# A two-layer transformer trunk: layer 1's projections in products of 256 columns, and an earlier wide product in layer 0

## The chip, the cores and the metric

The kernel runs on one core of a Trainium2 chip. TensorE (PE) does the matrix products, VectorE (DVE) and ScalarE (ACT) prepare their operands and finish their results, GpSimd (POOL) does small powers and sums, and SyncE (SP) issues the loads. The metric is the device time of one execution in microseconds (us); three runs of the kernel before gave a median of 558.01 us (557.69 to 558.17).

## The reference

Two layers over 256 tokens of width 1024, in float32. Layer 0 is a latent attention with a rotary key, layer 1 a block attention with a relative bias; each is followed by a squared-ReLU MLP:

```python
for i in range(DEPTH):                     # DEPTH = 2
    h = rms_norm(x, attn_norm[i])
    x = x + (mla_mixer(h, ...) if i % 2 == 0 else moba_mixer(h, w_qkv, ...))
    h = rms_norm(x, mlp_norm[i])
    x = x + sq_relu_mlp(h, w_in[i], w_out[i])     # relu(h @ w_in)**2 @ w_out

# moba_mixer, layer 1: all 256 tokens are one block, so it is causal attention with a bias
qkv = (h @ w_qkv).reshape(B, S, 3, 8, 128)
q, k = rms_norm(qkv[:, :, 0], q_norm), rms_norm(qkv[:, :, 1], k_norm)
out = attention(q, k, qkv[:, :, 2], rel_bias) @ w_o
```

## The kernel before

**Three products for one.** Every float32 operand is split into a rounded high part and a low remainder, and `mm3` multiplies high by high, low by high and high by low into the same PSUM bank. For weights the split is the work of two engines: `hi` makes the high part `wh` with a copy on ACT (line 169), `lo` subtracts it from the loaded weights on DVE and gives `wl` (line 178). `hTh` and `hTl` are the two parts of a layer's input h, transposed; `aT` those of the attention's output.

**Units and the ring.** The weights come as 185 units of up to 128x1024 in one fixed order. A unit is loaded by SP into one of 4 raw buffers, then split; `wh` and `wl` have 7 buffers each. `done(i)` says that unit i has been read for the last time, and `hi` goes no further than unit `used + 7`: where the ring is full, `hi` does nothing, and the `lo` that would follow has nothing to do either. `fill(n)` is `lo(n)` and then `hi(n)`. `unit(i)` splits on demand what is not split yet. Since a program's order on an engine is the order in which the code is written, where a `fill` stands decides what is queued behind the split on DVE and ACT.

**Layer 1's projections.** q, k and v are made in two halves of four heads each, so there are six groups, k0, q0, v0, k1, v1 and q1, of four units each, and each group has two rows, one for 128 tokens. A row is 24 products of 128x512 into one bank: eight k of the contraction by the three terms, with a part of h as the stationary operand and a part of the unit as the moving one. The two rows of k0 run side by side over k, with a `fill` at each second k and a `done` behind it. q0's first row follows directly, then `tok_sums` (four products of 2 columns, the tokens' sums of squares), q0's second row, transposes of k0, and so on: from there on, transposes or attention products stand between most rows. After `tok_sums` DVE and POOL make the tokens' scale, the roots of each head's sum of squares (POOL, line 270) and the normalised rows (DVE, line 352).

**Wide products.** `wider` makes the first product of some groups 258 columns wide instead of 256, the two more going into unused columns of the bank. A group gets one where TensorE has done another type of product before it (in the MLP), and output column block 5 of each attention (`(d, h) == (5, 0)`, line 646). The attention's output projection goes by column blocks d: blocks 0 to 3 are accumulated head by head (`o`), block 4 in pieces between them, blocks 5 to 7 at the end (`col`). Its last part is written as

```python
        o(6)
        fill()
        col(4, [4, 5, 6])
        o(7)
        col(4, [7])
        for d in range(5, KD):
            col(d, range(H))
```

Of the kernel before, what the change touches and what calls it, by code (L numbers as in the profile page):

```python
# [18 lines left out]
P = 128  # L19
# [4 lines left out]
S = 256  # L24
NT = S // P
KD = D // P
H = 8
# [33 lines left out]
def trunk(ctx: ExitStack, tc: tile.TileContext, A, out):  # L61
# [9 lines left out]
    def ps():  # L71
        return psum.tile([P, 512], F32, name="ps", tag="ps")
# [11 lines left out]
    def mm(o, a, b, start, stop):  # L84
        nc.tensor.matmul(o, a, b, start=start, stop=stop)  # L85

    def mm3(o, a, b, start, stop, wide=None, between=None):

        for i, (w, t) in enumerate(((0, 0), (1, 0), (0, 1))):
            if wide and i == 0:  # L90
                mm(wide[0], a[w], wide[1], start, False)
            else:
                mm(o, a[w], b[t], start and i == 0, stop and i == 2)
            if between and between[0] == i:
                between[1]()
# [7 lines left out]
    def wider(bank, b):  # L103
        moved[0] = True
        return bank[:, :S + 2], flat(b[:, :2])[:, :S + 2]
# [8 lines left out]
    def flat(ap):  # L114
        return ap.rearrange("p a b -> p (a b)")
# [20 lines left out]
    Q0 = len(units)  # L136
# [24 lines left out]
    def hi(n=1, eng=nc.scalar):  # L161

        for _ in range(n):
            i = len(his)
            if i < min(used[0] + RING, len(units)):
                load_raw()
                w = units[i][1]
                his.append(wsp.tile([P, 1024], F32R, name="wh", tag="wh"))
                (eng.copy if eng is nc.scalar else eng.tensor_copy)(his[i][:, :w], raws[i][:, :w])  # L169

    def lo(n=1, eng=nc.vector):

        for _ in range(n):
            i = len(los)
            if i < len(his):
                w = units[i][1]
                los.append(wsp.tile([P, 1024], F32R, name="wl", tag="wl"))
                eng.tensor_sub(los[i][:, :w], raws[i][:, :w], f32(his[i][:, :w]))  # L178
                load_raw()

    def fill(n=1):
        lo(n)
        hi(n)
# [7 lines left out]
    def unit(i):  # L191
        while len(his) <= i:
            hi()
        while len(los) <= i:
            lo()
        return his[i], los[i]

    def done(i):

        used[0] = max(used[0], i + 1)  # L200

    def part(u, sl):
        return u[0][:, sl], u[1][:, sl]
# [6 lines left out]
    x = const.tile([P, KD, S], F32)  # L210
# [72 lines left out]
    def hT(k, sl=slice(None)):  # L283
        return hTh[:, k, sl], hTl[:, k, sl]

    class SumSquares:


        def __init__(self):
            self.tot = work.tile([P, 2, S], F32, name="ssum", tag="ssum", bufs=1)  # L290
            self.prev = None
# [38 lines left out]
    class Norm:  # L330
# [19 lines left out]
        def rows(self, tok):  # L350
            self.y = t2(self.nh, self.width)
            nc.vector.scalar_tensor_tensor(self.y, self.p.rearrange("p (a b) -> p a b", b=self.width), tok,
                                           self.rs[:, :, None].to_broadcast([P, self.nh, self.width]),
                                           op0=OP.mult, op1=OP.mult)
# [201 lines left out]
    class Head:  # L556


        def __init__(self, hd, aT, h, bias, extra=None):
            self.aT = (aT[0][:, h], aT[1][:, h])  # L560
            self.two = aT[0][:, :2]
            self.i = h % HG
            self.hd = hd[h // HG]
            self.h, self.bias, self.extra = h, bias, extra
# [28 lines left out]
        def turn(self):  # L593
            pt = ps()
            for i in range(3):
                nc.tensor.transpose(pt[:, i * P:(i + 1) * P], self.p[:, i * P:(i + 1) * P], ident)  # L596
            self.pT = work.tile([P, 3 * P], F32, name="pT", tag="pT", bufs=3)
            nc.scalar.copy(self.pT, pt[:, :3 * P])
# [15 lines left out]
    def out_residual(a, d, gname):  # L614
        nc.vector.tensor_add(x[:, d], a, x[:, d])
        make_h_filled(d, gname)

    def run_heads(hs, proj, post, rows, turn, mid, base, gname, n1):

        A_ = [h.logits for h in hs]  # L620
        W_ = [h.weights for h in hs]
        B_ = [h.turn for h in hs]
        C_ = [h.values for h in hs]
        accs = []

        def o(h, ds=range(4)):
            u = unit(base + h // 2)
            for d in ds:
                if h == 0:
                    accs.append(ps()[:, :S])  # L630
                c = (h % 2) * 512 + d * P
                mm3(accs[d], part(u, slice(c, c + P)), hs[h].aT, h == 0, h == H - 1)
                if h == H - 1:
                    out_residual(accs[d], d, gname)
            if h % 2:
                done(base + h // 2)

        late = {}

        def col(d, hh):  # L640
            if d not in late:
                late[d] = ps()
            u = unit(base + d)
            for h in hh:
                mm3(late[d][:, :S], part(u, slice(h * P, (h + 1) * P)), hs[h].aT, h == 0, h == H - 1,
                    wider(late[d], hs[h].two) if (d, h) == (5, 0) else None)
            if hh[-1] == H - 1:
                done(base + d)
                out_residual(late[d][:, :S], d, gname)

        if mid is not None:
            proj("k1", 0)
            fill(n1)
            post("k1", 0)
            mid()
            proj("k1", 1)
            lo(n1)
            rows("k1", 0)
            hi(n1)
            post("k1", 1)  # L660
        A_[0]()
        proj("v1", 0)
        if mid is not None:
            lo(n1)
            rows("k1", 1)
        W_[0]()
        hi(n1)
        post("v1", 0)
        turn("k1", 0)
        A_[1]()  # L670
        if mid is None:
            rows("k1", 1)
        B_[0]()
        proj("v1", 1)
        lo(n1 + (mid is None))
        W_[1]()
        hi(n1)
        post("v1", 1)
        turn("k1", 1)
        C_[0]()  # L680
        A_[2]()
        B_[1]()
        proj("q1", 0)
        lo(n1)
        W_[2]()
        hi(n1)
        post("q1", 0)
        C_[1]()
        A_[3]()
        B_[2]()  # L690
        proj("q1", 1)
        lo(n1)
        W_[3]()
        rows("q1", 0)
        hi(n1)
        post("q1", 1)
        C_[2]()
        B_[3]()
        o(0)
        fill()  # L700
        turn("q1", 0)
        rows("q1", 1)
        C_[3]()
        o(1)
        fill()
        turn("q1", 1)
        o(2, range(2))
        A_[4]()
        o(2, range(2, 4))
        W_[4]()  # L710
        A_[5]()
        lo()
        o(3)
        B_[4]()
        hi()
        W_[5]()
        A_[6]()
        col(4, [0, 1])
        C_[4]()
        B_[5]()  # L720
        W_[6]()
        A_[7]()
        lo()
        col(4, [2, 3])
        C_[5]()
        B_[6]()
        hi()
        W_[7]()
        o(4)
        fill()  # L730
        C_[6]()
        B_[7]()
        o(5)
        fill()
        C_[7]()
# [7 lines that stand above are left out]
# [9 lines left out]
    open_p = {}  # L752
# [81 lines left out]
    heads_ctx, hd, aT = head_tiles(0)  # L834
# [16 lines left out]
    for o, a, b in rope_halves(m[:, :, 0], m[:, :, 1]):  # L851
        a, b = (i[:, :, None, :].to_broadcast([P, NT, 2, HALF]) for i in (a, b))
# [221 lines left out]
    for i, bs in enumerate(pairs):  # L1074
        at = 5 * i + 9
# [13 lines left out]
    order1 = {"k0": 0, "q0": 1, "v0": 2, "k1": 3, "v1": 4, "q1": 5}  # L1089
# [18 lines left out]
        tk = slice(t * P, (t + 1) * P)  # L1108
        to_T(norms[name, t].y, hd1[int(name[1])][name[0]][:, :, tk], gqk[:, 1:2] if name[0] == "q" else None)

    def proj1_k(name, t, p, k):
        b = Q0 + 4 * order1[name]
        tk = slice(t * P, (t + 1) * P)
        mm3(p, hT(k, tk), part(unit(b + k // 2), slice((k % 2) * 512, (k % 2 + 1) * 512)), k == 0, k == KD - 1)

    def proj1(name, t):
        p = ps()
        for k in range(KD):
            proj1_k(name, t, p, k)
        if t == NT - 1:  # L1120
            done(Q0 + 4 * order1[name] + 3)
        open_p[name, t] = p

    for t in range(NT):
        open_p["k0", t] = ps()
    for k in range(KD):
        for t in range(NT):
            proj1_k("k0", t, open_p["k0", t], k)
        if k % 2:
            fill()  # L1130
            done(Q0 + k // 2)
    total = sums1[0].total()
    for t in range(NT):
        post1("k0", t, False)
    proj1("q0", 0)
    ss3 = small.tile([P, 1, NT], F32, name="ss3", bufs=1)
    tok_sums(ss3, [total], ps())
    r3[0] = row_scale("3", ss3[:, 0])
# [99 lines left out]
```

## Time and profile before

| what | value |
|---|---|
| median of three runs | 558.01 us |
| profiled execution, its own time | 558.17 us |
| its span, first to last instruction | 556.4 us |
| granted TensorE clock, mean over the span | 1.000 |
| TensorE busy | 551.4 us (99%) |
| DVE, ACT, POOL busy | 394.2, 303.3, 93.9 us |

The span is what the trace covers; the execution's own time is 1.8 us more. Matmuls overlap in the pipeline, so the time from one start to the next tells their pace, not the duration that stands in a row.

### The profile page before, as it was taken

What the parts mean: (1) busy time and instruction counts of PE and PEld (TensorE: products, weight loads), DVE (VectorE), ACT (ScalarE), POOL (GpSimd) and SP (SyncE); (2) the same over time, 40 slices, a digit from 0 to 9 for tenths busy, and PEclk for the clock granted to TensorE, in tenths of its full rate; (3) what the DMA queues carried; (4) which work ended last, traced back from release to release, by engine and by line L of the source; (5) the groups of instructions that cost most, each with busy time, mean ns of one, the idle gap of its engine ahead of it and who ended that gap; (6) DMA issues with size and microseconds to landing.
All of it is one profiled execution on the core that took longest, in us unless ns stands there. A gap on an engine that the chain in (4) does not pass through costs nothing.

```text
span 556.4 us, 10756 instructions
## 1 busy us (share of the span) xinstructions
PE 551.4 (99%) x4324; PEld 524.8 (94%) x4324; DVE 394.2 (71%) x654; ACT 303.3 (55%) x495; POOL 93.9 (17%) x108
## 2 busy tenths in 40 slices
PE   9999999999999999999999999999999999999997
PEld 6878999999999999999988888999999999999997
DVE  5998777688997689866668356777867653977630
ACT  5899675674533365435365465746856442655420
POOL 3892100032132000012133100000130311000100
PEclk9999999999999999999999999999999999999999
DMA  8833534686567376645455544344865764565800
GB/s 298 299 126 117 152 119 157 193 274 196 180 201 214 120 219 195 198 149 182 155 186 186 185 160 149 118 152 121 266 219 183 235 193 148 188 201 181 285 29 29
DMA packets 29186, 99.57 MB, mean 179 GB/s; under 512 B 3824, under 2 KB 4720, under 8 KB 29136
## 3 DMA queue, kind: packets, MB, share of 16 engines
q1 hardware_dynamic: 28656, 97.94, 54.5%
q0 software_dynamic: 336, 0.92, 0.4%
q8 instruction: 34, 0.56, 0.4%
q14 instruction: 16, 0.13, 0.1%
q10 hardware_dynamic: 144, 0.02, 0.0%
HBM read 97.82 MB, written 1.05 MB: 178 GB/s over the span
## 4 chain that ended last, share of the span: by engine, by line
PE 96%; DVE 1%; DMA 1%; SPq 1%; ACT 0%; issue 0%; DVEq 0%
PE ps L85 93%; PE ps L372 2%; DMA x<-in_xT 1%; PE ps L596 1%; DVE wl L178 1%; SPq L158 0%; SPq L230 0%; PE ps L512 0%; DVE hTl L280 0%; ACT hTh L279 0%; ACT wh L169 0%; SPq L234 0%; DVE t L1064 0%; DVE rr L408 0%; DVE rr L416 0%
## 5 line engine op out<-in xcount | busy, mean ns | idle before, releaser
L178 DVE TENSOR_TENSOR wl<-raw,wh 128x1024 fp32r<-128x1024 f32 x177 | 218.0, 1248 | 34.5 <-ACT wh L169 34.1
L169 ACT CAST wh<-raw 128x1024 fp32r<-128x1024 f32 x177 | 182.6, 1046 | 72.4 <-PE ps L85 55.4
L85 PE MATMUL ps<-a,wh 128*128 128x256 f32 x1024 | 175.0, 276 | 0.0
L85 PEld LDWEIGHTS ps<-a,wh 128*128 128x128 f32 x1024 | 154.5, 188 | 0.0
L85 PE MATMUL ps<-hTl,wh 128*128 128x256 f32 x512 | 141.7, 277 | 0.0
L85 PE MATMUL ps<-a,wl 128*128 128x256 f32 x512 | 141.7, 277 | 0.0
L85 PE MATMUL ps<-hTh,wl 128*128 128x256 f32 x512 | 141.4, 276 | 0.0
L85 PE MATMUL ps<-hTh,wh 128*128 128x256 f32 x512 | 141.3, 276 | 0.0
L85 PEld LDWEIGHTS ps<-hTl,wh 128*128 128x128 f32 x512 | 96.1, 188 | 0.1
L85 PEld LDWEIGHTS ps<-hTh,wh 128*128 128x128 f32 x512 | 96.1, 188 | 0.1
L85 PEld LDWEIGHTS ps<-a,wl 128*128 128x128 f32 x512 | 96.1, 188 | 0.0
L85 PEld LDWEIGHTS ps<-hTh,wl 128*128 128x128 f32 x512 | 96.1, 188 | 0.0
L931 ACT ACTIVATE t<-ps 128x512 f32<-128x512 f32 (+1 forms) x34 | 19.5, 572 | 63.5 <-PE ps L85 63.5
L85 PE MATMUL ps<-aT,wh 128*128 128x256 f32 (+1 forms) x256 | 50.4, 288 | 0.0
L933 DVE SCALAR_TENSOR_TENSOR t<-ps,t 128x512 f32<-128x512 f32 (+1 forms) x34 | 22.4, 659 | 36.5 <-ACT t L931 36.3
L85 PE MATMUL ps<-wh,hTh 128*128 128x512 f32 (+2 forms) x128 | 46.0, 386 | 0.2 <-ACT wh L169 0.2
L85 PE MATMUL ps<-wl,hTh 128*128 128x512 f32 (+2 forms) x128 | 45.2, 378 | 0.4 <-DVE wl L178 0.4
L85 PE MATMUL ps<-wh,hTl 128*128 128x512 f32 (+2 forms) x128 | 45.0, 377 | 0.0
L85 PEld LDWEIGHTS ps<-aT,wh 128*128 128x128 f32 x256 | 40.4, 188 | 0.2
L85 PE MATMUL ps<-aT,wl 128*128 128x256 f32 x128 | 35.6, 278 | 0.0
L609 ACT ACTIVATE hTh<-x,gains 128x256 fp32r<-128x256 f32 x24 | 12.2, 510 | 42.3 <-POOL x L1055 25.8
L270 POOL TENSOR_TENSOR hrs<-hss,mhalf 128x4 f32<-128x4 f32 (+1 forms) x18 | 23.2, 1297 | 65.4 <-DVE hss L347 48.8
(167 smaller groups left out, 624.2 us busy)
## 6 DMA issues: line engine op xcount, KB each, us to landing
raw<-in_w_in_mlp SPq DMA_DIRECT2D x64, 512.0 KB, 4.4
raw<-in_w_out_mlp SPq DMA_DIRECT2D x64, 512.0 KB, 4.3
raw<-in_w_qkv SPq DMA_DIRECT2D x24, 512.0 KB, 3.8
raw<-in_w_u SPq DMA_DIRECT2D x8, 512.0 KB, 6.1
win<-in_w_in SPq DMA_DIRECT2D x8, 352.0 KB, 5.5
raw<-in_w_o0a SPq DMA_DIRECT2D x4, 512.0 KB, 3.9
raw<-in_w_o0b SPq DMA_DIRECT2D x4, 512.0 KB, 3.5
raw<-in_w_o1a SPq DMA_DIRECT2D x4, 512.0 KB, 4.0
```

The lines of the kernel that those rows point to most:

```text
L85: nc.tensor.matmul(o, a, b, start=start, stop=stop)
L169: (eng.copy if eng is nc.scalar else eng.tensor_copy)(his[i][:, :w], raws[i][:, :w])
L178: eng.tensor_sub(los[i][:, :w], raws[i][:, :w], f32(his[i][:, :w]))
L270: nc.gpsimd.tensor_tensor(dst, t, mhalf[:, :n].rearrange("p (a b) -> p a b", b=t.shape[-1]) if len(t.shape) == 3 else mhalf[:, :n], op=OP.pow)
L372: nc.tensor.transpose(pt[:, i * P:(i + 1) * P], yf[:, i * P:(i + 1) * P], ident)
L596: nc.tensor.transpose(pt[:, i * P:(i + 1) * P], self.p[:, i * P:(i + 1) * P], ident)
L609: nc.scalar.activation(hTh[:, k], x[:, k], AF.Copy, scale=gain(gname, k))
L931: nc.scalar.activation(rl, src, AF.Relu)
L933: nc.vector.scalar_tensor_tensor(sq, src, 0.0, rl, op0=OP.max, op1=OP.mult)
```

## The change

Each product of 512 columns in layer 1's projections becomes two of 256, with the same stationary part and the two halves of the same bank. In the first rows, k0's pair and q0's first, one product (of k = 3, with the low part of h) is taken out of its place: its first half is done in seventh place and is 258 columns wide, its second half has the other 254 and comes last. Since that last one still reads k0's second unit, `done` for k0's second and third unit moves to the end of the k0 rows. In layer 0 alone, the wide product of column block 5 is gone; block 4 has two, for head 0 (the first of the block) and for head 5 (the fourth product of its piece for heads 4, 5 and 6). Layer 1's attention keeps the wide product of block 5.

```diff
-            self.two = aT[0][:, :2]
+            self.two = aT[0][:, h:h + 2] if h < H - 1 else None
...
+                wide = d == 4 and h in (0, 5) if mid is None else (d, h) == (5, 0)
                 mm3(late[d][:, :S], part(u, slice(h * P, (h + 1) * P)), hs[h].aT, h == 0, h == H - 1,
-                    wider(late[d], hs[h].two) if (d, h) == (5, 0) else None)
+                    wider(late[d], hs[h].two) if wide else None)
...
-        mm3(p, hT(k, tk), part(unit(b + k // 2), slice((k % 2) * 512, (k % 2 + 1) * 512)), k == 0, k == KD - 1)
...
+    def proj1_row(todo, wide=False):
+        kick, rest = (todo[0][:2] + (3, 1, half) if wide else None for half in range(2))
+        if wide:
+            todo = [x for x in todo if x not in (kick, rest)]
+            todo = todo[:6] + [kick] + todo[6:] + [rest]
+        last = {x[:2]: x for x in todo}
+        for x in todo:
+            name, t, k, i, half = x
+            c0, c1 = (0, S + 2) if x == kick else (S + 2, 2 * S) if x == rest else (half * S, (half + 1) * S)
+            w = unit(Q0 + 4 * order1[name] + k // 2)[i // 2][:, (k % 2) * 512 + c0:(k % 2) * 512 + c1]
+            mm(open_p[name, t][:, c0:c1], hT(k, slice(t * P, (t + 1) * P))[i % 2], w, (k, i, half) == (0, 0, 0),
+               x == last[name, t])
+            yield
...
-    for k in range(KD):
-        for t in range(NT):
-            proj1_k("k0", t, open_p["k0", t], k)
-        if k % 2:
+    row = [("k0", t, k, i, half) for k in range(KD) for t in range(NT) for i in range(3) for half in range(2)]
+    for at, _ in enumerate(proj1_row(row, True), 1):
+        if at % 24 == 0:
             fill()
-            done(Q0 + k // 2)
+            if at in (24, 96):
+                done(Q0 + at // 24 - 1)
...
-    proj1("q0", 0)
+    proj1("q0", 0, True)
```

On TensorE, at the start of the k0 rows, before (`ps_3610` is the last bank of layer 0's MLP, `ps_3692` and `ps_3693` are the banks of k0's two rows, `wh_3484` is k0's first unit):

```order
L85 MATMUL ps_3610<-a1_1324,wh_3448 128x256
L85 MATMUL ps_3692<-wh_3484,hTh_156 128x512
L85 MATMUL ps_3692<-wh_3484,hTl_157 128x512
L85 MATMUL ps_3692<-wl_3486,hTh_156 128x512
L85 MATMUL ps_3693<-wh_3484,hTh_156 128x512
```

and of the change (`wh_3524` is k0's second unit):

```order
L85 MATMUL ps_3610<-a1_1324,wh_3448 128x256
L85 MATMUL ps_3692<-wh_3484,hTh_156 128x256 x2
L85 MATMUL ps_3692<-wh_3484,hTl_157 128x256 x2
L85 MATMUL ps_3692<-wl_3486,hTh_156 128x256 x2
L85 MATMUL ps_3692<-wh_3524,hTl_157 128x258
L85 MATMUL ps_3693<-wh_3484,hTh_156 128x256 x2
```

Each product has become two, and the wide one stands seventh. There are 288 products of 512 columns before and 576 of half the width in the change.

On DVE, from the sums of the tokens on (`ss3`), before; `wl_3813` is the second unit of v0, `wl_3857` and `wl_3903` are its third and fourth, and its first stands in the k0 rows already; the three L352 are the normalised rows of k0, k0 and q0, and the second L343 belongs to q0's second row:

```order
L316 COPY ss3_3796<-ps_3797 128x2
L347 TENSOR_SCALAR hss_3768<-hss_3768,sq3_3805 128x4
L178 TENSOR_TENSOR wl_3813<-raw_3669,wh_3760 128x1024
L343 TENSOR_REDUCE hss_3820<-t2_3819 128x4
L347 TENSOR_SCALAR hss_3820<-hss_3820,sq3_3805 128x4
L352 SCALAR_TENSOR_TENSOR t2_3851<-ps_3692,rs_3_3803,hrs_3807 128x512
L352 SCALAR_TENSOR_TENSOR t2_3853<-ps_3693,rs_3_3803,hrs_3810 128x512
L352 SCALAR_TENSOR_TENSOR t2_3855<-ps_3771,rs_3_3803,hrs_3823 128x512
L178 TENSOR_TENSOR wl_3857<-raw_3722,wh_3817 128x1024
L343 TENSOR_REDUCE hss_3866<-t2_3865 128x4
L347 TENSOR_SCALAR hss_3866<-hss_3866,sq3_3805 128x4
L178 TENSOR_TENSOR wl_3903<-raw_3740,wh_3861 128x1024
```

and of the change, where `wl_3943`, `wl_3947`, `wl_3999` and `wl_4015` are v0's four units:

```order
L316 COPY ss3_3860<-ps_3861 128x2
L347 TENSOR_SCALAR hss_3808<-hss_3808,sq3_3869 128x4
L343 TENSOR_REDUCE hss_3882<-t2_3881 128x4
L347 TENSOR_SCALAR hss_3882<-hss_3882,sq3_3869 128x4
L352 SCALAR_TENSOR_TENSOR t2_3937<-ps_3692,rs_3_3867,hrs_3871 128x512
L352 SCALAR_TENSOR_TENSOR t2_3939<-ps_3693,rs_3_3867,hrs_3874 128x512
L352 SCALAR_TENSOR_TENSOR t2_3941<-ps_3811,rs_3_3867,hrs_3885 128x512
L178 TENSOR_TENSOR wl_3943<-raw_3639,wh_3877 128x1024
L178 TENSOR_TENSOR wl_3947<-raw_3669,wh_3879 128x1024
L343 TENSOR_REDUCE hss_3956<-t2_3955 128x4
L347 TENSOR_SCALAR hss_3956<-hss_3956,sq3_3869 128x4
L178 TENSOR_TENSOR wl_3999<-raw_3746,wh_3951 128x1024
```

Two `fill`s of the k0 rows find the ring full, so v0's first two subtractions stand behind the three normalised rows instead of in the k0 rows and in front of the reduction, and all of the units after them come up to two places later in DVE's order.

On TensorE in layer 0's output projection, of the change (`ps_1032` is block 4, `ps_892` the first of the next four):

```order
L85 MATMUL ps_904<-aT1_478,wh_912 128x256
L85 MATMUL ps_1032<-aT0_477,wh_943 128x256
L85 MATMUL ps_1032<-aT0_477,wl_992 128x256
L85 MATMUL ps_1032<-aT1_478,wh_943 128x256
L85 MATMUL ps_1032<-aT0_477,wh_943 128x258
L85 MATMUL ps_1032<-aT0_477,wl_992 128x256
```

Before, all of these are 128x256, and the first of 258 comes 21 products further on, as the first into block 5's bank.

## Rows read from the trace of the kernel before

**Rows 1.** The page: busy time, granted clock in 40 slices, the chain by engine.

```profile
PE 551.4 (99%) x4324; PEld 524.8 (94%) x4324; DVE 394.2 (71%) x654; ACT 303.3 (55%) x495; POOL 93.9 (17%) x108
...
PEclk9999999999999999999999999999999999999999
...
PE 96%; DVE 1%; DMA 1%; SPq 1%; ACT 0%; issue 0%; DVEq 0%
```

**Rows 2.** TensorE in order of time, layer 0's last output blocks: start, duration, what.

```profile
81.20 0.28 PE L85 MATMUL ps<-aT,wl 128*128 128x256 f32 x1
...
85.09 0.28 PE L85 MATMUL ps<-aT,wl 128*128 128x256 f32 x1
...
85.79 0.28 PE L85 MATMUL ps<-aT,wl 128*128 128x256 f32 x1
...
93.27 0.28 PE L85 MATMUL ps<-aT,wl 128*128 128x256 f32 x1
```

**Rows 3.** Groups of instructions: TensorE's products of 258 columns, with their counts.

```profile
L85 PE MATMUL ps<-a,wh 128*128 128x258 f32 x4 | 1.1, 280 | 0.0
...
L85 PE MATMUL ps<-hTh,wh 128*128 128x258 f32 x3 | 0.8, 280 | 0.0
...
L85 PE MATMUL ps<-aT,wh 128*128 128x258 f32 x2 | 0.6, 280 | 0.0
```

**Rows 4.** TensorE in order of time: first of k0's rows, tok_sums, q0's second row.

```profile
271.70 0.39 PE L85 MATMUL ps<-wh,hTh 128*128 128x512 f32 x1
...
288.49 0.50 PE L85 MATMUL ps<-ones,ssum 128*128 128x2 f32 x4
288.85 0.48 PE L85 MATMUL ps<-wh,hTh 128*128 128x512 f32 x1
```

**Rows 5.** TensorE in order of time: the transposes of k0, v0's first row.

```profile
294.53 1.03 PE L372 MATMUL ps<-ident,t 128*128 128x128 f32 x8
295.32 0.48 PE L85 MATMUL ps<-wh,hTh 128*128 128x512 f32 x1
```

**Rows 6.** TensorE in order of time: two stretches of 256 columns after other products.

```profile
75.08 0.28 PE L85 MATMUL ps<-aT,wl 128*128 128x256 f32 x1
...
75.42 0.28 PE L85 MATMUL ps<-aT,wl 128*128 128x256 f32 x1
...
76.54 0.36 PE L85 MATMUL ps<-aT,wh 128*128 128x256 f32 x1
...
78.04 0.81 PE L85 MATMUL ps<-pT,v 128*128 128x256 f32 x4
```

**Rows 7.** DVE in order of time, from the k0 rows to v0's first row.

```profile
280.83 4.39 DVE L178 TENSOR_TENSOR wl<-raw,wh 128x1024 fp32r<-128x1024 f32 x3 [0.97 <-ACT wh L169]
...
290.67 1.21 DVE L178 TENSOR_TENSOR wl<-raw,wh 128x1024 fp32r<-128x1024 f32 x1
...
292.82 0.75 DVE L352 SCALAR_TENSOR_TENSOR t<-ps,rs,hrs 128x512 f32<-128x512 f32 x1
...
294.74 0.75 DVE L352 SCALAR_TENSOR_TENSOR t<-ps,rs,hrs 128x512 f32<-128x512 f32 x1 [0.23 <-POOL hrs L270]
295.41 1.22 DVE L178 TENSOR_TENSOR wl<-raw,wh 128x1024 fp32r<-128x1024 f32 x1
296.54 0.68 DVE L343 TENSOR_REDUCE hss<-t 128x4 f32<-128x512 f32 x1
...
297.39 1.22 DVE L178 TENSOR_TENSOR wl<-raw,wh 128x1024 fp32r<-128x1024 f32 x1
```

**Rows 8.** POOL in order of time: the first root, then the other two.

```profile
290.71 2.08 POOL L270 TENSOR_TENSOR hrs<-hss,mhalf 128x4 f32<-128x4 f32 x1 [0.54 <-DVE hss L347]
...
292.73 1.98 POOL L270 TENSOR_TENSOR hrs<-hss,mhalf 128x4 f32<-128x4 f32 x2
```

**Rows 9.** DVE and TensorE in order of time, block 4 of layer 1's output projection.

```profile
356.45 1.22 DVE L178 TENSOR_TENSOR wl<-raw,wh 128x1024 fp32r<-128x1024 f32 x1
...
357.56 0.28 PE L85 MATMUL ps<-aT,wl 128*128 128x256 f32 x1
```

More of the change, by code (lines that the diff above doesn't have):

```diff
@@ L1109, in turn1, with proj1 @@
         to_T(norms[name, t].y, hd1[int(name[1])][name[0]][:, :, tk], gqk[:, 1:2] if name[0] == "q" else None)
-    def proj1_k(name, t, p, k):
-        b = Q0 + 4 * order1[name]
-        tk = slice(t * P, (t + 1) * P)
-        mm3(p, hT(k, tk), part(unit(b + k // 2), slice((k % 2) * 512, (k % 2 + 1) * 512)), k == 0, k == KD - 1)
-    def proj1(name, t):
-        p = ps()
-        for k in range(KD):
-            proj1_k(name, t, p, k)
+    def proj1_row(todo, wide=False):
[11 more added lines that the diff above has]
+            yield
+    def proj1(name, t, wide=False):
+        open_p[name, t] = ps()
+        for _ in proj1_row([(name, t, k, i, half) for k in range(KD) for i in range(3) for half in range(2)], wide):
+            pass
         if t == NT - 1:
             done(Q0 + 4 * order1[name] + 3)
-        open_p[name, t] = p
     for t in range(NT):
         open_p["k0", t] = ps()
-    for k in range(KD):
-        for t in range(NT):
-            proj1_k("k0", t, open_p["k0", t], k)
-        if k % 2:
+    row = [("k0", t, k, i, half) for k in range(KD) for t in range(NT) for i in range(3) for half in range(2)]
+    for at, _ in enumerate(proj1_row(row, True), 1):
+        if at % 24 == 0:
             fill()
-            done(Q0 + k // 2)
+            if at in (24, 96):
+                done(Q0 + at // 24 - 1)
     total = sums1[0].total()
```

## The prediction

> **What bounds the kernel now.** I read the page first: TensorE works 99% of the span at a granted clock of 1.0 in all 40 slices, and 96% of the chain that ended last is TensorE's [rows 1]. So the change is worth what it does to the spacing of TensorE's products, and every wait that it puts into their stream counts in full; time saved on another engine counts nothing. Next I took TensorE in order of time and looked at starts only, since durations overlap. Products of 256 columns have two paces. In layer 0's last output blocks, the 33 products from 81.20 to 85.09 take 3.89 us, 117.9 ns each; the 66 from 85.79 to 93.27 take 7.48, 113.3 ns each [rows 2]. Between the two stands a product of 258 columns. The trace has nine of them (4 + 3 + 2) [rows 3], and I looked at each: from the second product behind it on the pace is 113.3 every time, and it stays through changes of bank, operand and part of the MLP until another type of product comes. Behind one the pace is 117.9: 12 products from 76.54 to 78.04 take 1.50 us, a first gap of 0.20 and eleven of 0.118. One short stretch, from 75.08 to 75.42, has three in 0.34 without any wide product in front [rows 6]; of some 25 stretches it is the only one. Products of 512 have one pace: 72 of them, from 271.70 to 288.49, take 16.79 us, 233.2 ns each [rows 4]. So two of 256 save 6.5 ns against one of 512 at the quick pace and lose 2.6 at the slow one. Last I read DVE and POOL around layer 1's first rows, because the weights' subtractions move there.
>
> **The change part by part.** The sum is made on the profiled execution, 558.17 us, of which 556.4 are the span; it lies 0.16 above the median, 558.01.
>
> *Layer 0's wide product.* It stands in 16th place behind the last other product instead of 37th, in a stream that was slow and that the nine cases say will turn quick. 21 products x 4.6 ns = 0.10 us less. The other new one, first in block 4, has five products behind it before another type comes: 0.02 at most, taken as nothing. Both read two columns of the next head's output, which the same products' neighbours read already, so they wait for nothing new.
>
> *k0's rows and q0's first row.* 72 products of 512 become 144. The stream before k0 is the MLP's, quick since its last wide product, and k0's first product waits for nothing there. 144 x 113.3 ns = 16.32, and some 0.03 for two wide products and their rests of 254: 16.35 against 16.79, 0.44 less. What a wide product does in a stream that is quick already, no row shows: all nine came in slow ones. Bounds: nothing, or the pace is lost for the rest of k0 (89 x 4.6 ns = 0.41 more), until q0's own, then in a slow stream, brings it back. I take nothing, since nothing but another type of product ever ended the quick pace. k0's wide product needs the second unit a few us early; it was split before the row begins.
>
> *The other nine rows.* q0's second, v0, k1, v1 and q1 with two each. One row takes 5.68 us now, from 288.85 to 294.53 [rows 4, 5]. As 48 products behind other work, with a first gap of 0.20 and 47 x 117.9 ns, it takes 5.74: 0.06 more, nine times 0.56. The other bound is the quick pace, 0.20 + 47 x 113.3 = 5.53, 0.15 less per row. These rows have activations as the stationary part and use each twice running, which no 256-column row of the trace does; I take the slow end, which all but one of the stretches show.
>
> *The subtractions.* Before, v0's first unit is subtracted in the k0 rows, the third of a run of three [rows 7], and its second between the roots. In the change both stand behind the three normalised rows, so I count from tok_sums, T (288.49 before). There the first root on POOL begins at T + 2.22 and takes 2.08, the other two 1.98 together, 1.0 each [rows 8]. Beside the long one runs the subtraction of v0's second unit, 290.67 to 291.88 [rows 7]; 1.0 us after its end the root is done. I read it as a root held up by DVE, so that without this subtraction it takes 1.0 too. The Trainium skill says so as well: a DVE instruction with two SBUF inputs contends with a GpSimd instruction that reads SBUF, and the second to start blocks ("SBUF — State Buffer", Who interferes with whom); the trace's 2.08 against 1.0 agrees.
>
> Then the roots end at T + 5.14, the third normalised row starts 0.03 later, and the first subtraction 0.67 behind it (294.74 to 295.41 [rows 7]), at T + 5.84. It takes 1.22, two in a row start 1.14 apart: ready at 7.06 and 8.20. TensorE reaches v0 at T + 0.36 + 5.74 + 0.79 (eight transposes [rows 5]) = 6.89, and its fifth product, the first that reads a remainder, at 7.45: 0.4 of slack. The third unit comes behind the reduction of q0's second row, 0.85 from its start to the subtraction's (296.54 to 297.39 [rows 7]): started at 8.11 + 0.85 = 8.96, ready at 10.18, wanted 24 products after the first, at 10.28. The fourth is ready at 11.31, wanted at 11.69. So nothing to 0.3 us of waiting; I take 0.05. Queued behind these on DVE are q0's second row, wanted only after k1's first, and the remainders of k1, ready some 5 us early by the same count. SP's loads for k1 go out behind the subtractions that free the raw buffers, and k1 is some 19 us behind T: no cost. On ACT two splits move behind the squares of k0, which therefore run earlier; nobody waits for either.
>
> *One more place.* The units stay a place behind until the MLP. In layer 1's output projection the subtraction from 356.45 on is then that of block 4, whose second product starts at 357.56 [rows 9]: ready at 357.67, with a start behind it 0.15 late.
>
> Sum: -0.10 - 0.44 + 0.56 + 0.05 + 0.15 = +0.22, so 558.39 on the profiled execution and 558.23 on the median. I forecast 558.3 us.
>
> **The rivals.** *The products don't turn quick* (the change doesn't do what it says): k0 and q0 run at 117.9, 144 x 117.9 = 16.98 in place of 16.35, or k0 alone loses the pace. The total is 558.7 to 558.9. For it: the operands' new roles, a wide product in a quick stream; against: nine of nine.
> The Trainium skill's spacing of N/2.4 + 2.5 ns ("TensorE: Matmul & The Clock Gate", Back-to-back issue gap) speaks for it: every halved product would cost 2.5 ns more, 288 x 2.5 = 0.72 us, estimated from that page. The rows have 20 ns over 512 columns' own 213.3 and not 2.5, so it doesn't hold here.
>
> *All nine other rows run quick.* Then they save 9 x 0.15 = 1.35 in place of losing 0.56; TensorE comes to v0's third unit at T + 9.95, 0.25 before it is ready, so the wait is 0.29. 558.01 - 0.10 - 0.44 - 1.35 + 0.29 + 0.15 = 556.6. For it: one stretch that turned quick by itself, and stationary parts used twice; against: all the others.
>
> *v0 waits for its remainders* (slower). If the first root takes 2.08 whatever runs beside it, the three subtractions come 1.08 later: the first is ready at T + 8.14, 0.7 after TensorE wants it, and the third another 0.3 later than wanted, 1.0 in all. The total is 559.2 to 559.3. It decides once the first subtraction ends later than T + 7.45. For it: the order has put them there, and 0.4 us is a small margin; against: the other two roots took 1.0.
>
> **How the numbers follow.** About 0.2% (1.1 us) is what a measurement of this kernel can tell from no change. The forecast has 0.50, the slow products 0.21, quick rows 0.14, the wait at v0 0.15. The first two lie within 0.2%; the third is faster by 0.25%; the fourth is slower by 0.22%, near the line, and may stay inside. So faster 0.14, same 0.73, slower 0.13. The forecast's own range is 557.8 to 558.7; the range reaches to the quick rows at 556.6 and to v0's wait at 559.3.
>
> **What would show it.** In the changed profile: products from k0's first to tok_sums at 113.3 ns, 16.35 us in all; rows of 5.74 us behind transposes; the pace in layer 0 turning behind block 4's wide product; a first root of 1.0 us; TensorE without a gap in v0's first row; a gap of 0.15 at block 4 of layer 1. I am wrong if a row behind transposes takes 5.53, if the wide product ends the quick pace, or if DVE shows in TensorE's waits in v0.

## The result and the profile after

The changed kernel takes 564.48 us (564.11 to 564.61, four runs); the kernel before, beside it, 557.85 (557.57 to 558.17). The ratio is 1.0117 [1.0102, 1.0131]: 6.6 us slower, where 0.3 slower was forecast and the range ended at 559.3. The profiled execution of the change took 564.11 us, its span 562.3.

The page of the changed kernel answers to [rows 1]: busy time, granted clock in 40 slices, the chain by engine.

```profile
PE 557.0 (99%) x4612; PEld 543.8 (97%) x4612; DVE 394.7 (70%) x654; ACT 302.4 (54%) x495; POOL 90.5 (16%) x108
...
PEclk9999999999999999999999999999999999999999
...
PE 96%; DVE 1%; DMA 1%; SPq 1%; issue 0%; ACT 0%; DVEq 0%
```

No share here shows the 6 us: no lower clock, no new wait in the chain, TensorE at 99% as before. So the time is in the pace of the products again, and that is read from starts.

TensorE of the change in order of time, layer 0's last output blocks (start, duration, what), answers to [rows 2]:

```profile
80.94 0.28 PE L85 MATMUL ps<-aT,wl 128*128 128x256 f32 x1
...
82.35 0.28 PE L85 MATMUL ps<-aT,wl 128*128 128x256 f32 x1
...
82.70 0.28 PE L85 MATMUL ps<-aT,wl 128*128 128x256 f32 x1
...
92.91 0.28 PE L85 MATMUL ps<-aT,wl 128*128 128x256 f32 x1
```

12 products take 1.41 us ahead of the wide one (between the second row and the third), 117.5 ns each; 90 take 10.21 behind it, 113.4. It turns the stream in its new place, as forecast.

The same view of layer 1's first rows and of block 4 of its output projection, for [rows 4, 5, 9]:

```profile
271.33 0.40 PE L85 MATMUL ps<-wh,hTh 128*128 128x256 f32 x2
...
272.04 0.28 PE L85 MATMUL ps<-wh,hTl 128*128 128x258 f32 x1
...
282.15 0.28 PE L85 MATMUL ps<-wh,hTl 128*128 128x254 f32 x1
...
282.97 0.28 PE L85 MATMUL ps<-wh,hTl 128*128 128x258 f32 x1
...
287.75 0.50 PE L85 MATMUL ps<-ones,ssum 128*128 128x2 f32 x4
288.11 0.49 PE L85 MATMUL ps<-wh,hTh 128*128 128x256 f32 x2
...
293.67 1.04 PE L372 MATMUL ps<-ident,t 128*128 128x128 f32 x8
294.46 0.48 PE L85 MATMUL ps<-wh,hTh 128*128 128x256 f32 x2
...
297.61 0.40 PE L85 MATMUL ps<-wh,hTl 128*128 128x256 f32 x2
298.03 0.51 PE L85 MATMUL ps<-wl,hTh 128*128 128x256 f32 x2
298.38 0.40 PE L85 MATMUL ps<-wh,hTh 128*128 128x256 f32 x2
...
355.92 0.47 PE L85 MATMUL ps<-aT,wh 128*128 128x256 f32 x1
356.39 0.39 PE L85 MATMUL ps<-aT,wl 128*128 128x256 f32 x1
356.61 0.40 PE L85 MATMUL ps<-aT,wh 128*128 128x256 f32 x2
...
364.78 0.36 PE L85 MATMUL ps<-aT,wh 128*128 128x256 f32 x1
```

and of the kernel before, around the second product of block 4 in [rows 9]:

```profile
357.25 0.47 PE L85 MATMUL ps<-aT,wh 128*128 128x256 f32 x1
...
357.68 0.40 PE L85 MATMUL ps<-aT,wh 128*128 128x256 f32 x2
...
365.93 0.36 PE L85 MATMUL ps<-aT,wh 128*128 128x256 f32 x1
```

k0's rows and q0's first take 16.42 us (271.33 to 287.75) in place of 16.79. q0's second row, behind `tok_sums`, takes 5.56 (288.11 to 293.67) in place of 5.68. In v0's first row two pairs of products start 0.42 apart, where the others stand 0.24 apart: a wait of 0.18 at the first use of the third unit's remainder, 298.03. The next pair follows after 0.35, 0.11 more, so the wait costs 0.29. At block 4 the first and second product stand 0.47 apart, before 0.31, and the second and third 0.22, before 0.12: a wait that costs 0.27. By the start of the last long stretch the change is ahead: its first product stands at 364.78, before at 365.93. Of these 1.15 us, 0.29 are there already at the first edited product (71.48, before 71.77); that much differs between profiled executions of the same products too, so the edits have gained 0.86.

Then it loses everything. The table by stretches (us, TensorE's busy time and number of products, and so on to the granted clock, DMA share and GB/s), first of the kernel before:

```profile
380.00:415.00 35.00, 35.00 (x311) 35.00 (x310) 25.46 (x32) 23.26 (x34) 6.65 (x4) 1.00 0.67 217
420.00:550.00 130.00, 130.00 (x1149) 130.00 (x1148) 78.57 (x88) 54.19 (x62) 11.81 (x15) 1.00 0.54 174
```

and of the change:

```profile
380.00:415.00 35.00, 35.00 (x299) 35.00 (x299) 24.33 (x29) 23.00 (x33) 6.56 (x4) 1.00 0.64 211
420.00:550.00 130.00, 130.00 (x1106) 130.00 (x1106) 79.09 (x88) 54.73 (x62) 10.31 (x14) 1.00 0.56 173
```

The same stretch of time, the same work, a granted clock of 1.00 in both, and 43 products fewer in 130 us. With two products taken off that already run at the start of a stretch, the pace is 113.3 ns before and 117.8 in the change. The wide products of layer 1's block 5 (at 369.11) and of its MLP (at 417.60) are both there, and neither turns the stream. I call these two the late wide products from here on, and say that one works where it turns the stream. 403 + 1198 products x 4.45 ns = 7.1 us lost, 1.15 gained up to there: 6.0 net, where the two profiled executions differ by 5.94.

### The profile page after: what moved, and what is told of

It reads as the page before. It is cut to its first block, busy times and chain, and to the rows that moved or that the text cites. A ratio compares the mean times of both kernels' runs of the same rounds, so it can differ in the third digit from the quotient of the medians.

```text
span 562.3 us, 11331 instructions
## 1 busy us (share of the span) xinstructions
PE 557.0 (99%) x4612; PEld 543.8 (97%) x4612; DVE 394.7 (70%) x654; ACT 302.4 (54%) x495; POOL 90.5 (16%) x108
## 4 chain that ended last, share of the span: by engine, by line
PE 96%; DVE 1%; DMA 1%; SPq 1%; issue 0%; ACT 0%; DVEq 0%
PE ps L85 93%; PE ps L372 1%; DMA x<-in_xT 1%; PE ps L596 1%; DVE wl L178 1%; SPq L158 0%; SPq L230 0%; PE ps L512 0%; DVE hTl L280 0%; ACT wh L169 0%; ACT hTh L279 0%; SPq L234 0%; DVE t L1066 0%; DVE rr L408 0%; PE ps L882 0%
## 5 line engine op out<-in xcount | busy, mean ns | idle before, releaser
L85 PE MATMUL ps<-a,wh 128*128 128x256 f32 x1024 | 178.5, 278 | 0.0
L85 PE MATMUL ps<-aT,wh 128*128 128x256 f32 x256 | 50.7, 289 | 0.0
L85 PE MATMUL ps<-wh,hTh 128*128 128x256 f32 (+2 forms) x224 | 45.7, 289 | 0.5 <-DVE wh L446 0.5
L85 PE MATMUL ps<-wl,hTh 128*128 128x256 f32 (+2 forms) x224 | 45.0, 285 | 0.4 <-DVE wl L178 0.4
L85 PE MATMUL ps<-wh,hTl 128*128 128x256 f32 (+2 forms) x224 | 45.0, 285 | 0.0
L85 PEld LDWEIGHTS ps<-wh,hTh 128*128 128x128 f32 x224 | 34.4, 188 | 1.1 <-ACT hTh L279 1.0
L85 PEld LDWEIGHTS ps<-wl,hTh 128*128 128x128 f32 x224 | 34.5, 188 | 1.0 <-DVE wl L178 0.9
```

## The experiments

Three theories at first. *Place in the program*: a wide product works or not by where its instruction stands, and 288 more products moved it. *Late units*: the ring, one unit behind since k0's rows, makes the weights late. *Phase*: a slow stream has an inner rhythm, and a wide product turns it only where it hits it rightly.

**Layer 0's edit alone.** The kernel before, with

```diff
-            self.two = aT[0][:, :2]
+            self.two = aT[0][:, h:h + 2] if h < H - 1 else None
...
+                wide = d == 4 and h in (0, 5) if mid is None else (d, h) == (5, 0)
...
-                    wider(late[d], hs[h].two) if (d, h) == (5, 0) else None)
+                    wider(late[d], hs[h].two) if wide else None)
```

> The kernel before with only layer 0's two new wide products. Theories of the 6.1 us that the changed kernel lost (its two wide products in layer 1's block 5 and in layer 1's MLP left the stream at 118 ns, where before they turned it to 113.3). Phase: a wide product turns the slow stream only if the stream meets it in a certain phase, set by what TensorE did since it last stood still; this edit moves what comes behind by 0.1 us, and the later wide products may work or not, each on its own: 557.8 if all work, about 560 if layer 1's block 5 alone fails (409 products x 4.6 ns = 1.9), about 563 if the MLP's alone fails (1198 x 4.6 ns = 5.5). Place in the program: no instruction more than before, so all work: 557.8 us. Late units: the ring is as before, all work: 557.8 us. So 557.8 says nothing against any, and takes layer 0's edit out of the causes.

558.14 us against 558.17, ratio 0.9999 [0.9989, 1.0008]. Both late wide products work. Layer 0's edit is not the cause.

**Layer 1's rows alone.** The change, with

```diff
-                wide = d == 4 and h in (0, 5) if mid is None else (d, h) == (5, 0)
+                wide = (d, h) == (5, 0)
```

> The changed kernel with layer 0's wide product put back into block 5. Phase: layer 0's edit comes 290 us ahead of the failing place, and layer 1's rows lie between; the two late wide products fail as in the change, 564.5 us, or one of them works again (562.6 with block 5 turned, 559.0 with the MLP turned), or both (about 557). Place in the program: the same 578 more instructions as in the change, both fail: 564.5 us. Late units: the ring lags as in the change, both fail: 564.5 us. If both work, the cause is something that layer 0's edit carries along.

564.34 us, ratio 1.0109 [1.0093, 1.0126]: the whole loss comes with the rows.

**The rows without their wide products.** The change, with

```diff
-    for at, _ in enumerate(proj1_row(row, True), 1):
+    for at, _ in enumerate(proj1_row(row), 1):
...
-            if at in (24, 96):
-                done(Q0 + at // 24 - 1)
+            done(Q0 + at // 24 - 1)
...
-    proj1("q0", 0, True)
+    proj1("q0", 0)
```

> The changed kernel without the wide products of k0's and q0's rows, with each unit given free where it was before, so that the ring does not fall behind. Late units: the two late wide products work again, about 557 us (or 557.5 if k0's rows stay at 118 ns). Place in the program: still 576 more instructions than before, both fail: 564.5 to 565 us. Phase: the start of the late stretch moves by some tenths of a us, so either may turn: 557, 559, 562.6 or 564.5 us. k0's rows tell as well whether they turn quick by themselves: 16.3 us from k0's first product to the tokens' sums if so, 17.0 if not.

557.51 us, ratio 0.9987 [0.9977, 0.9996]. Both late wide products work, with as many products in front of them as in the change: place in the program, as a count of products, falls. Late units and phase stand. k0's rows and q0's first take 16.97 us here, so without a wide product they stay slow.

**More wide products.** The change, with

```diff
-                wide = d == 4 and h in (0, 5) if mid is None else (d, h) == (5, 0)
+                wide = d == 4 and h in (0, 5) if mid is None else d > 4 and h == 0
...
-                    if k == f == 0 and not moved[0]:
+                    if k == f == 0 and (not moved[0] or (l, r) == (1, 0) and j < 4):
```

> The changed kernel with more wide products in layer 1: the first product of blocks 6 and 7 besides block 5, and the first product of the first four groups of the MLP's second part. Phase: each further one meets the stream in another phase, and one of them will turn it: about 557.2 us or below, and the stream stays quick from there on even where another wide product follows. Place in the program: they stand at other places, and some may work too, so 557 to 564. Late units: the weights are on time by blocks 6 and 7, and these work: about 557.2. If all fail, 564.5 us, and it is not the phase of single wide products.

564.68 us, ratio 1.0114 [1.0099, 1.0129]: seven in the last stretch ahead of the tokens' sums, three in blocks 5 to 7 and four in the MLP's groups behind them, and none turns it. That looked fatal for phase, until I averaged the gaps of the slow streams, from the trace's starts in nanoseconds, by their place modulo three. A slow stream is not even: two gaps of 117.5 ns and one of 118.3 repeat. The seven stand 24 or 48 products apart, multiples of three, so all seven met the same place. Beside the wide product's own gap and the next three, for block 5 (the first column: mean gap of the products 3, 6, 9 ... ahead of it; then 1, 4, 7 ...; then 2, 5, 8 ...; all in ns):

```
                      3,6,9..  1,4,7..  2,5,8..   its own gap, next three   turned
before                 118.36   117.33   117.67   119  117 114 113          yes
rows without wides     118.36   117.33   117.67   119  117 114 113          yes
change                 117.45   118.50   117.33   118  120 122 118          no
layer 1's rows alone   117.73   118.33   117.33   118  120 122 117          no
```

Where the wide product stands in the long place it turns the stream; right behind a long one it does not. The next runs test this by shifting the wide product alone.

**One product more, and two, ahead of block 5.** The change, with `range(1)` and with `range(2)` in

```diff
+            if mid is not None and d == 5:
+                for _ in range(1):
+                    mm(late[d][:, S:], part(u, slice(0, P))[0], hs[0].aT[0], True, True)
             for h in hh:
```

> The changed kernel with one more product of 256 columns (0.12 us, into unused columns of the same bank) just ahead of layer 1's block 5, so that block 5's wide product comes one place later in the slow stream. What the runs so far show: a slow stream has a period of three products, two gaps of 117.5 ns and one of 118.3; wide products that turned it stood in the long place (three back, six back, ... is long), those that failed stood right behind the long one, and all that failed stood there, because they lie multiples of three apart. Phase of three: the place right ahead of the next long one has not been tried; the wide product either turns the stream there (557.2 + 0.1 = 557.3 us) or not (564.6 us). Place in the program or late units: it fails again, 564.6 us.

> The changed kernel with two more products of 256 columns ahead of layer 1's block 5 (0.24 us), so that its wide product stands in the long place of three. Phase of three: it turns the stream, block 5 to the end of the MLP's second part run at 113.3, and the MLP's later wide product works too: 564.5 - 7.2 + 0.2 = 557.5 us. Place in the program (by any even count) or late units: it fails, 564.7 us.

With two: 557.47 us where 557.5 was expected, ratio 0.9989 [0.998, 0.9999]. With one: 559.27, ratio 1.002 [1.001, 1.003], between the two values expected. The stretches with two more products,

```profile
380.00:415.00 35.00, 35.00 (x311) 35.00 (x310) 25.66 (x31) 23.27 (x33) 6.57 (x4) 1.00 0.69 218
420.00:550.00 130.00, 130.00 (x1149) 130.00 (x1148) 78.05 (x88) 53.97 (x61) 11.84 (x15) 1.00 0.55 174
```

and with one:

```profile
380.00:415.00 35.00, 35.00 (x300) 35.00 (x299) 24.21 (x30) 22.75 (x34) 6.70 (x4) 1.00 0.69 216
420.00:550.00 130.00, 130.00 (x1149) 130.00 (x1149) 79.86 (x90) 55.76 (x64) 11.30 (x14) 1.00 0.55 175
```

With two the stream is quick in both. With one, block 5's wide product fails (300 products), the MLP's works (1149): I had not expected these to part. The slow stream's place carries over the two products of the tokens' sums that stand ahead of the MLP's wide product. In the four kernels in which that one fails, the long gap is two back from the slow stream's last product; in the four in which it works out of a slow stream, one back. The first gap behind the sums differs too, 307 or 308 ns in the four that fail and 305 in the other ten.

**One product more in the kernel before**, the mirror: the same lines, added to the kernel that works.

> The kernel before with one more product of 256 columns ahead of layer 1's block 5 and nothing else, so that its wide product leaves the long place for the one right behind it. Phase of three: the wide product fails, 409 products run 4.6 ns longer (1.9 us), and the MLP's late wide product, which comes out of a slow stream as in the change, fails too (1198 x 4.6 ns = 5.5): 557.9 + 0.1 + 1.9 + 5.5 = 565.4 us, or 559.9 if the MLP's works. So one product of 0.12 us costs 7.4 us. Place in the program or late units: nothing but the product itself, 558.0 us.

565.61 us where 565.4 was expected, ratio 1.0133 [1.0118, 1.0148]:

```profile
380.00:415.00 35.00, 35.00 (x299) 35.00 (x299) 23.74 (x29) 22.55 (x33) 7.01 (x4) 1.00 0.64 214
420.00:550.00 130.00, 130.00 (x1106) 130.00 (x1106) 79.97 (x89) 55.81 (x64) 10.21 (x14) 1.00 0.56 173
```

One product of 0.12 us costs 7.4, and the loss of the change is made with nothing of the change in the kernel. What was left: why did the change move the stream out of phase?

**The rest in its old place, the units on time.** The change, with

```diff
-            todo = [x for x in todo if x not in (kick, rest)]
-            todo = todo[:6] + [kick] + todo[6:] + [rest]
+            todo = [x for x in todo if x != kick]
+            todo = todo[:6] + [kick] + todo[6:]
...
-            if at in (24, 96):
-                done(Q0 + at // 24 - 1)
+            done(Q0 + at // 24 - 1)
```

> The changed kernel with the 254-column rest of the two wide products of layer 1's first rows done in its old place, not last, and every unit given free where it was before; so the wide products are there and the ring does not fall behind. It asks what set the phase of the late stretch in the change. Late units and the wait at block 4: gone, the late wide products work, and k0's and q0's rows are quick up to the rest: 557.0 us. The wide products themselves, by what they add to the rows: the late ones fail, 564.5 us. By chance alone: one in three for each place.

Eight of ten executions took 556.97 to 558.07 us, two 564.24 and 565.04; median 557.7, ratio 1.0011 [0.9977, 1.0046], unclear by itself. The profiled one has both late wide products working. The two long ones lie 6.5 and 7.3 us above the median, near the 7.1 that both late wide products cost where they fail; so the place seems not to be the same in every execution here, but there is no trace of a long one. In the profiled one the rests of 254 columns throw k0's and q0's rows back to 117.8 ns, from 276.56 and 285.72 on. It also shows an exception to the place of three: q0's wide product, at 283.99, stands right behind the long gap (118.3 ns, the other places 117.4 and 117.7), and from the fifth product behind it on the stream is quick all the same. In these rows each stationary part is used twice running, and the rule of three is shown only for streams in which it changes with every product.

**The units caught up.** The change, with

```diff
     post1("v0", 1)
+    fill()
     run_heads([Head(hd1, aT1, h, bias[:, h]) for h in range(H)], proj1, post1, rows1, turn1, lambda: turn1("q0", 1), O1, "mlp1", 2)
```

> The changed kernel with one more fill behind v0's second row, which brings the units back to the places that they had before; the rows with their wide products, and all products of TensorE, stay as in the change. It asks what moved the late stream out of phase. Late units: the wait of 0.17 us more at layer 1's block 4 is gone, the stretch before block 5 starts as before (first gap 202 ns, long gap in the wide product's own place), both late wide products work: 564.5 - 7.2 - 0.2 = 557.1 us. The rows (their pace, their wide products): the stream stays out of phase, 564.3 us. One in three by chance.

557.12 us where 557.1 was expected, ratio 0.998 [0.9971, 0.9989], the ten runs within 0.57 us. One `fill`, which moves work of DVE and ACT alone and leaves TensorE's 4612 products and their order as they are, gives back 7.4 us. TensorE at block 4, and the stretches:

```profile
356.17 0.47 PE L85 MATMUL ps<-aT,wh 128*128 128x256 f32 x1
356.47 0.28 PE L85 MATMUL ps<-aT,wl 128*128 128x256 f32 x1
```

```profile
380.00:415.00 35.00, 35.00 (x311) 35.00 (x311) 25.17 (x30) 22.38 (x32) 6.56 (x4) 1.00 0.68 216
420.00:550.00 130.00, 130.00 (x1150) 130.00 (x1149) 77.39 (x87) 54.02 (x61) 11.80 (x15) 1.00 0.54 174
```

The two products of block 4 stand 0.30 apart again, the wide product of block 5 is back in the long place (118.36, 117.33, 117.67), and this version is 0.2% below the kernel before.

The traces show part of the way from block 4 to the wide product, and it divides all fourteen kernels into two sevens. With late units, block 4's first two gaps are 472 to 479 and 221 to 227 ns; with units on time, 305 or 306 and 117 or 118. In the attention products that follow, the second product of probabilities by v (`ps<-pT,v`, at 361.82 in the change and 362.88 before) starts 215 ns behind the first with late units and 284 to 290 with units on time: a wait of 0.07 us that the late TensorE no longer meets. And the last long stretch opens with a gap of 204 or 205 ns with late units, of 202 with units on time; counted from there, the long place is the same within each seven, and one place apart between them. The run with the rest in its old place is counted by its profiled execution.

**A wider product in the bad place.** The change, with 4 and with 8 columns more in place of 2 for layer 1's block 5:

```diff
-    def wider(bank, b):
+    def wider(bank, b, n=2):
         moved[0] = True
-        return bank[:, :S + 2], flat(b[:, :2])[:, :S + 2]
+        return bank[:, :S + n], flat(b[:, :2])[:, :S + n]
...
-                    wider(late[d], hs[h].two) if wide else None)
+                    wider(late[d], hs[h].two, 2 if mid is None else 4) if wide else None)
```

> The changed kernel with layer 1's block-5 wide product of 260 columns in place of 258, in the same bad place. What the runs so far show: a wide product turned the stream where its own gap came to 119.2 ns (long place, 118.3 + 0.8), and failed where it came to 118.3 (short places, 117.5 + 0.8). If the length of the gap decides, 260 columns make 117.5 + 1.7 = 119.2 in the short place, and the stream turns: 557.3 us. If the place of three decides, whatever the width: 564.5 us.

> The same with 264 columns, 3.3 ns more than 256: a gap of 120.8 ns in the short place. If a gap of 119.2 or more decides: 557.3 us. If the place decides: 564.5 us. If the gap must be 119.2 within less than a tick (more is as bad as less): 564.5 us here and 557.3 with 260 columns.

559.0 us, ratio 1.0014 [1.0004, 1.0023], and 559.01, 1.0016 [1.0006, 1.0025]. Block 5 stays slow with either: the gaps are 119, 117, 116, 121 ns with 260 columns, 121, 117, 117, 119 with 264. So a gap of 119 does not do it; of the two expectations the place decides. The total is not the 564.5 that this expected: behind the wider product the rhythm has shifted by one place, the long gap ahead of the tokens' sums is one back instead of two, and the MLP's wide product works.

**Wide products in a quick stream.** The kernel before, with

```diff
-                    wider(late[d], hs[h].two) if (d, h) == (5, 0) else None)
+                    wider(late[d], hs[h].two) if (d, h) == (5, 0) or mid is not None and d > 5 and h == 0 else None)
```

> The kernel before with two more wide products, as the first of layer 1's blocks 6 and 7, where the stream is quick already (the prediction found no row for this and took it as free). Phase: the quick stream has gaps of 113.3 ns and, with nothing that waits in it, nothing to fall out of: 558.0 us, nothing lost. If a wide product throws a quick stream back as a product of 254 columns did in the change's first rows: 385 products or so at 117.8 until the MLP's wide product, 1.8 us, 559.8; with that failing as well 565.3 us.

559.66 us where 559.8 was expected for a throw-back, ratio 1.0027 [1.0016, 1.0039]. Block 6's wide product, in the quick stream, has the gaps 114, 118, 120, 118, and the stream is slow from there to the MLP's wide product. Block 7's, which stands right ahead of the long place, does not turn it:

```profile
380.00:415.00 35.00, 35.00 (x300) 35.00 (x299) 23.92 (x30) 22.40 (x33) 7.07 (x4) 1.00 0.67 214
420.00:550.00 130.00, 130.00 (x1150) 130.00 (x1149) 79.97 (x90) 55.82 (x64) 11.27 (x14) 1.00 0.55 175
```

## Why the prediction was wrong, step by step

**Layer 0's wide product** (-0.10): measured -0.09 there and 0.02 lost behind the other one, first in block 4, which turns nothing. It was right by luck. The 21 products by which the wide product moved are a multiple of three, so it stands in the long place again (118.5 ns three, six and more back, the other places 117.4); the prediction knew of no such place.

**k0's rows and q0's first** (-0.44): measured -0.37. Two steps inside were wrong and small. k0's first products run at 118 ns although the MLP's stream was quick, so its wide product met a slow stream and was needed. And "nothing but another type of product ever ended the quick pace" fell: the 254 at 282.15 did, and in the last experiment a wide product did.

**The other nine rows** (+0.56, the slow end of the bounds): wrong side. All nine, v0's waits included, take 50.54 us after 51.16, 0.62 less. Seven are quick, six of them by themselves within some six products and one from the row ahead of it; q1's first stays slow (5.74 us), v0's first is slow up to its wait. I had weighed one quick stretch against some 24 slow ones, and put aside the one thing that these rows do differently, each stationary part used twice running. Whether that is why they turn quick, no run tests. The rival with nine quick rows makes the edits 1.45 us faster up to 364.78, the forecast 0.22 slower; measured are 0.86 faster, nearer to the rival.

**The subtractions** (+0.05): the mechanism held, the wait costs 0.29. DVE and POOL of the change from the roots on, for [rows 7, 8]:

```profile
293.64 2.35 DVE L178 TENSOR_TENSOR wl<-raw,wh 128x1024 fp32r<-128x1024 f32 x2
...
296.76 2.35 DVE L178 TENSOR_TENSOR wl<-raw,wh 128x1024 fp32r<-128x1024 f32 x2
```

```profile
289.98 2.96 POOL L270 TENSOR_TENSOR hrs<-hss,mhalf 128x4 f32<-128x4 f32 x3 [0.54 <-DVE hss L347]
...
296.93 1.91 POOL L270 TENSOR_TENSOR hrs<-hss,mhalf 128x4 f32<-128x4 f32 x1 [3.99 <-DVE hss L347]
```

Without a subtraction beside it the first root takes 1.0 us (three in 2.96), as worked out; the next, beside the subtraction of 296.76, takes 1.91. This is the contention that the Trainium skill describes ("SBUF — State Buffer", Who interferes with whom), on this side of the change too. The third subtraction ends near 297.98 (296.76 and 1.22), and TensorE starts on it at 298.03: the bound for quick rows, 0.29, was met, though v0's first row was slow up to there.

**One more place** (+0.15): 0.27 at block 4, since the product behind the late one comes late as well, and 0.07 of it is got back at the next products by v, so 0.20. What else follows from it was not in the sum.

**The step that failed** stands in the first part, "from the second product behind it on the pace is 113.3 every time", and in what I left out: the late wide products of layer 1 are not touched by the diff, so they were taken as they were. Nine of nine was the count of a kernel in which all nine stand where they work; it was no rule. A wide product turns the slow stream of block 5 in one place of three. The ring that falls one unit behind in k0's rows makes block 4's remainder late, TensorE loses 0.27 us there, the last long stretch starts otherwise, and block 5's wide product comes right behind the long gap. It costs 403 products their pace, and the slow stream hands the MLP's wide product a bad place too: 1198 more, 7.1 us in all. Two products more in the change and one more in the kernel before show that the place decides, the caught-up ring that lateness moved it; each came within 0.3 us of the time expected. No rival held this: where I asked what a wait costs, I counted its length, not what it does to a stream that depends on when it starts.

**Still open.** Why the rhythm has three places, and why a stretch that opens with 205 ns has its long place elsewhere than one that opens with 202, no run shows; that the wait of block 4 itself, and nothing else that late units bring, makes that first gap is argued from the order of the rows. Nor does any run tell why the time varied from execution to execution with the rest in its old place.

## What to carry to other kernels

When a kernel's pace hangs on a trick whose condition isn't known, every instance of it is a term of every later change, even where the diff doesn't touch it: look for what decides it before counting how often it worked, and look at the untouched ones first when a result is off. A wait is priced twice, by its length and by what it does to the stream behind it; here 0.27 us of waiting cost 7.1 more. And where a count says "always", ask whether the cases were chosen: a tuned kernel shows only the places that work.

## What the runs showed of the hardware

- A stream of 256-column float32 products has two paces at the same granted clock of 1.00 (2.4 GHz): 113.3 ns, even, and 117.8 ns, in threes of 117.5, 117.5 and 118.3. Behind the MLP's late wide product either lasted over some 1200 products. The quick pace was lost without a product of another width at k0's first product, where activations become the stationary part (gaps of 113 ns, then 117 to 119).
- In layer 1's last stretch one product of 258 columns turned the slow pace into the quick one in the long place of three in seven of seven kernels. Right behind the long place it failed in ten of ten tries, right ahead of it in two of two; 260 and 264 columns, tried right behind, failed too. In a quick stream one of 258 did the reverse, as products of 254 did.
- Where each stationary part is used for two products running, a stream behind other work turned quick by itself in most of the change's rows, and the one wide product there with a readable bad place turned the stream all the same. Halving products of 512 columns (233.2 ns) saved time in quick streams alone: k0's rows and q0's first took 16.79 us whole, 16.42 mostly quick, 16.97 slow.
- The place of three seems to outlive a short interruption: across the two products of the tokens' sums it went with the next wide product's success in eight of eight kernels. No run moved that wide product by itself.
